# Branch B's scores: the second product of each head on 64 rows, side by side for two heads

## The chip, the cores and the metric

The kernel runs on one core of a Trainium2 chip. The metric is the time of one execution in microseconds of device time (median of the runs). Inputs and output are float32; TensorE gets its operands as float32r, split into a high part (rounded to float32r) and a low part (the remainder), so that a product of two values is made of several matmuls.

## The reference

One block of a bidirectional encoder, 1024 tokens of width 1024 and 16 meta tokens in front. Two attention branches read one normed input: branch A, differential attention over all tokens, and branch B, grouped-query attention in a window, with a sink logit for each head. Gates merge them, and a SwiGLU feed-forward follows. The change is in branch B's scores:

```
# 8 heads in 2 groups (g) of 4 (r), one key head per group, head width d = 64
s = einsum('bnqgrd,bnkgd->bngrqk', q, k) * d**-0.5 - slope * distance   # a block of 128 queries
s = where(visible, s, -inf)                                             # 3 blocks of keys + 16 meta keys
m = maximum(max(s), sink); p = exp(s - m)
y = einsum('bngrqk,bnkgd->bnqgrd', p / (sum(p) + exp(sink - m)), v)
```

## The kernel before

All engines' instructions are put in order by a scheduler that simulates the program when it is built; later stages fix TensorE's order by hand. The stages are: the input is loaded, normed and transposed (`turn_x`, through `transposed`, L154 to L165), with the first projections among the transposes; branch B's attention, woven into the projections of the rest (`project_steps`, L230); branch A's attention, woven into the gate projections (L881); then output projection and feed-forward. TensorE runs one instruction after another in the order that was built, so branch B's products stand between projection matmuls.

Branch B works on one group `g` and one tile `t` of 128 queries at a time (`attend_b`, L382): 2 groups by 8 tiles, 4 heads `r` in each. The keys of a tile are three blocks of 128 with the 16 meta keys behind each, 432 columns; the first and the last tile have two blocks, 288 columns.

Query and key have 64 values for each head, and the array has 128 rows, so high and low part share the rows. `qb[:, r]` holds the high part of head r's queries in rows 0 to 63 and the low part in rows 64 to 127. `kb[g][:, v]` holds the keys twice: for v = 0 high part above low part, for v = 1 low part above high part. Two matmuls of 128 rows, summed in one PSUM bank, thus give all four products of high and low parts. `kb_consume` (L305) and the `consume` of `qb_steps` (L367) copy the parts from a staging tile to these rows by DMA on SP's queue.

Each head's score goes to a bank of its own from a pair of banks under the tag "bs" (two buffers of one bank). VectorE's reduction (L399) adds the bias and takes the extreme value while it copies the score out; ScalarE's exponential (L403), GpSimd's scaling (L409), TensorE's transposes (L432) and the product with the values (L437) follow. `turn_x` uses the same two banks for the transposes of odd tiles, eight for each tile in two groups of four, and those of "bt" for the even tiles. The ninth tile holds the 16 meta tokens only, so its eight transposes have 16 rows.

Of the kernel before, what the change touches and what calls it, by code (L numbers as in the profile page):

```python
# [9 lines left out]
F32 = mybir.dt.float32  # L10
# [4 lines left out]
ALU = mybir.AluOpType  # L15
# [4 lines left out]
P = 128  # L20
# [54 lines left out]
def encoder_block(ctx: ExitStack, tc: tile.TileContext, x, meta, norm_mix, w_in, lq1, lk1, lq2, lk2,  # L75
                  subln, sink, w_ba, w_bb, w_o, norm_ffn, w_g, w_u, w_d, norm_final, out, dbg=None):
    nc = tc.nc
# [5 lines left out]
    def f32(ap):  # L83
        return ap.bitcast(F32)
# [13 lines left out]
    def bank(p, tag, name, bufs):  # L98
        return p.tile([P, 512], F32, tag=tag, name=name, bufs=bufs)
# [54 lines left out]
    def transposed(pp, xn, parts, hi, lo, at, name):  # L154

        highs = []
        for b in range(2):
            pt = pp(f"ptn_{name}_{b}").rearrange("p (c t) -> p c t", c=4)
            for c in range(4):
                k = 4 * b + c  # L160
                turned = nc.tensor.transpose(pt[:, c, :parts], xn[:parts, k * P:(k + 1) * P], ident[:parts, :parts])
            h = hi[:, 4 * b:4 * b + 4, at:at + parts]
            highs.append(nc.scalar.activation(h, pt[:, :, :parts], AF.Copy))
            low = nc.vector.tensor_tensor(lo[:, 4 * b:4 * b + 4, at:at + parts], pt[:, :, :parts], f32(h), ALU.subtract)
        return highs, low, turned  # L165
# [6 lines left out]
    psum1, close_psum1 = pool("psum1", space=PSUM)  # L172
# [4 lines left out]
    hT_hi = hpool.tile([P, DC, L_ROW], F32R, name="hT_hi")  # L177
    hT_lo = hpool.tile([P, DC, L_ROW], F32R, name="hT_lo")
# [33 lines left out]
    def ensure(n):  # L212
        while order and len(prepped) < n:
            col = order.pop(0)
            prepped[col] = prep(col, f"c{col}", lo_eng=nc.vector if col == C_QB else None)
# [73 lines left out]
    kb = [bpool.tile([P, 2, NT, 144], F32R, name=f"kb{g}") for g in range(BG)]  # L289
# [15 lines left out]
    def kb_consume(st, at, n):  # L305
        b0, nb = at // P, n // P
        for g in range(BG):
            rows = slice(64 * g, 64 * g + 64)
            for hl in range(2):
                for var, dst in ((0, slice(64 * hl, 64 * hl + 64)), (1, slice(64 - 64 * hl, 128 - 64 * hl))):  # L310
                    nc.sync.dma_start(f32(kb[g])[dst, var, b0:b0 + nb, 0:P],
                                      st[rows, hl, :nb * P].rearrange("p (b k) -> p b k", k=P))
                    if n % P:
                        nc.sync.dma_start(f32(kb[g])[dst, var, :, P:144],
                                          st[rows, hl, nb * P:n].unsqueeze(1).broadcast_to([64, NT, NM]))

    def vb_evac(pt, k0, nb, kp):
# [46 lines left out]
    def qb_steps(g, qb, jj):  # L364
        j = 2 * g + jj

        def consume(st, at, n):  # L367
            for par in range(2):
                for hl in range(2):
                    nc.sync.dma_start(f32(qb)[64 * hl:64 * hl + 64, 2 * jj + par, at:at + n],  # L370
                                      st[64 * par:64 * par + 64, hl, :n])
        return project_steps(C_QB + j * P, QB_CHUNKS if j < 2 else Q_CHUNKS, f"qb{j}", evac_split(qbs[:, j:j + 1], consume),
                             hi_first=j < 2)

    def project_qb(g, qb):
        for jj in range(2):
            ensure(1)
            for _ in qb_steps(g, qb, jj):
                pass
            ensure(W_BUFS - 1)  # L380

    def attend_b(g, t, qb):  # L382
        nm = f"{g}_{t}"
        b0, b1 = max(t - 1, 0), min(t + 2, NT)
        nb = b1 - b0
        W = nb * 144
        j0 = b0 - t + 1
        tb = tbx[:, j0:j0 + nb, :].rearrange("p j k -> p (j k)")
        st = bpool.tile([P, 4, 432], F32, tag="bs", name=f"bs_{nm}", bufs=2)
        mn = small.tile([P, 4], F32, tag="bmn", name=f"bmn_{nm}")  # L390
        dn = small.tile([P, 4], F32, tag="bdn", name=f"bdn_{nm}")
        es = small.tile([P, 4], F32, tag="bes", name=f"bes_{nm}")
        hs = slice(4 * g, 4 * g + 4)
        for r in range(4):
            ps = bank(psum1, "bs", f"bps_{nm}_{r}", 2)
            for v in range(2):
                nc.tensor.matmul(ps[:, :W], qb[:, r, t * P:(t + 1) * P],  # L397
                                 kb[g][:, v, b0:b1, :].rearrange("p b k -> p (b k)"), start=(v == 0), stop=(v == 1))
            nc.vector.tensor_tensor_reduce(st[:, r, :W], ps[:, :W], tb, 2.0 ** -(4 * g + r + 1), nsink[:, 4 * g + r:4 * g + r + 1],  # L399
                                           ALU.add, ALU.min, mn[:, r:r + 1])  # L400
        nc.vector.tensor_tensor(es, mn, sinkb[:, hs], ALU.add)
        for r in range(4):
            nc.scalar.activation(st[:, r, :W], st[:, r, :W], AF.Exp, bias=mn[:, r:r + 1], scale=-1.0,  # L403
                                 accum_out=dn[:, r:r + 1])
        nc.scalar.activation(es, es, AF.Exp)
        nc.vector.tensor_tensor(dn, dn, es, ALU.add)
        nc.vector.reciprocal(dn, dn)  # L407
        for r in range(4):
            scaled.append(nc.gpsimd.tensor_scalar(st[:, r, :W], st[:, r, :W], dn[:, r:r + 1], 1.0, ALU.mult, ALU.mult))  # L409

        md = mds[t % 2]
        own = (t - b0) * 144 + P
        nc.gpsimd.tensor_copy(md.rearrange("p (r a k) -> p r a k", r=4, a=2),
                              st[:, :, own:own + NM].unsqueeze(2).broadcast_to([P, 4, 2, NM]))

        def finish():
            py = bank(psum1, "by", f"bpy_{nm}", 1)
            for k in [8, *range(b0, b1)]:
                o = (k - b0) * 144
                pt = bank(psum1, "bt", f"bpt_{nm}_{k}", 2).rearrange("p (r t) -> p r t", r=4)  # L420
                if k == 8:
                    nc.tensor.transpose(pt[:, 0, :], md, ident)
                    tm = tms[t % 2]
                    hi = bpool.tile([P, P], F32R, tag="bmh", name=f"bmh_{nm}", bufs=1)
                    nc.scalar.activation(hi, pt[:, 0, :], AF.Copy, scale=of_hi)
                    for r in range(4):
                        at = slice(32 * r, 32 * r + 32)
                        nc.vector.scalar_tensor_tensor(tm[at, r], pt[at, 0, :], of_x[at], f32(hi[at]), ALU.mult, ALU.subtract)
                    nc.tensor.matmul(py, vb[g][:, 8, :], tm.rearrange("p r t -> p (r t)"), start=True, stop=False)
                    continue  # L430
                for r in range(4):
                    nc.tensor.transpose(pt[:, r, :], st[:, r, o:o + P], ident)  # L432
                tr = bpool.tile([P, 2, 4, P], F32R, tag="btr", name=f"btr_{nm}_{k}", bufs=4)
                nc.scalar.activation(tr[:, 0], pt, AF.Copy)
                nc.vector.tensor_tensor(tr[:, 1], pt, f32(tr[:, 0]), ALU.subtract)
                for hl in range(2):
                    nc.tensor.matmul(py, vb[g][:, k, :], tr[:, hl].rearrange("p r t -> p (r t)"),  # L437
                                     start=False, stop=(k == b1 - 1 and hl == 1))
            y1 = bpool.tile([64, 512], F32, tag="by1", name=f"by1_{nm}", bufs=2)
            nc.scalar.copy(y1, py[64:128])  # L440
            nc.vector.tensor_tensor(y1, py[0:64], y1, ALU.add)
            nc.sync.dma_start(yb_d[g][:, t * P:(t + 1) * P].rearrange("(r d) t -> d r t", r=4),
                              y1.rearrange("d (r t) -> d r t", r=4))
        return finish

    qb = new_qb(0)
# [6 lines left out]
    xts, xns, done, early = {}, {}, [], []  # L453
# [17 lines left out]

    def turn_x(t):
        parts = P if t < NT else NM
        return transposed(lambda name: bank(psum1, ("bt", "bs")[t % 2], name, 2), xns.pop(t), parts, hT_hi, hT_lo, t * P, f"a{t}")

    def advance(n):
        while n > 0 and early:
# [15 lines left out]
    rows = bpool.tile([DC, P], F32, tag="by1", name="gain_rows", bufs=2)  # L493
# [8 lines left out]
    for b in range(2):  # L502
        pt = pp_bank(f"gain_{b}")
        gain.append(pt)
        for c in range(4):
            k = 4 * b + c
# [14 lines left out]
    _, _, turned = turn_x(0)  # L521
# [4 lines left out]
    highs, low, _ = turn_x(1)  # L526
# [38 lines left out]
    product = advance(3 * DC)  # L565
# [4 lines left out]
    with tc.issue_after(product.ins):  # L570
        highs, _, _ = turn_x(4)
# [13 lines left out]
    highs, _, _ = turn_x(7)  # L585
    _, low, _ = turn_x(NT)
# [35 lines left out]
    nsink = acon.tile([P, BH], F32, name="nsink")  # L622
# [64 lines left out]
    for _ in range(QA_FIRST):  # L687
        product = next(qa0)
# [7 lines left out]
    qb = new_qb(1)  # L696
# [387 lines left out]
    for n in range(AH * NT + T_LAG):  # L1084
# [3 lines left out]
        if n < AH * NT:  # L1088
            h, t = divmod(n, NT)
# [178 lines left out]
    for o in range(DC):  # L1268
        w = first_w[o] if o < 2 else branch_w(ypool, o, w_bb, "b")
        for half in range(2):  # L1270
            gt, ps, tk = gated(0, o, half, w, yb)
# [599 lines left out]
```

## Time and profile before

| what | value |
|---|---|
| median of 3 runs | 1424.24 us (1422.53 to 1424.48) |
| the profiled execution | 1424.24 us, its span 1421.9 us |
| TensorE matmul busy | 1401.0 us, 99% of the span |
| VectorE, ScalarE, GpSimd busy | 914.8, 672.1, 636.7 us |
| branch B's score products (L397) | 128, from 62.1 to 269.7 us |

Rows of the timeline give an instruction's start and duration in us, engine, line, operation, output and inputs, the array's rows and columns in use (128\*128), the moving operand (128x432), and how many alike were merged (x2). PE is TensorE's matmul, PEld its weight load. A matmul's duration reaches into the next one's, as they are pipelined; the distance between starts says what one costs.

### The profile page before, as it was taken

The numbers are of one execution on the slowest core, as the hardware profiler recorded it, in microseconds if no ns is written. First come the engines' busy times: TensorE is split into PE (matmuls) and PEld (weight loads), VectorE is DVE, ScalarE is ACT, GpSimd is POOL, SyncE is SP. The second block draws the span as 40 slices with busy tenths as digits, with TensorE's granted clock in tenths as the row PEclk, the third lists the DMA queues.
The fourth block names the chain that finished last, engine by engine and source line by source line (L and its number), as shares of the span: only waits on it lengthen the run. The fifth ranks groups of instructions, "written<-read, shape, count | busy, mean of one in ns | idle before, by whom it ended". The sixth has DMA issues, their size and how long they took to land.

```text
span 1421.9 us, 20667 instructions
## 1 busy us (share of the span) xinstructions
PE 1401.0 (99%) x7183; PEld 1202.7 (85%) x7183; DVE 914.8 (64%) x1584; ACT 672.1 (47%) x1284; POOL 636.7 (45%) x648
## 2 busy tenths in 40 slices
PE   9999999998999999999999999999999999999998
PEld 8998999987888888878888888888888888888886
DVE  6555666527787878666978956544555453787566
ACT  6355556435445555455346644333333333444454
POOL 4156865546677666322503055555545441000442
PEclk9999999999999999999999999999999999999999
DMA  8446565386896363296522724433333323954343
GB/s 235 92 128 184 154 199 160 106 290 225 259 318 211 105 209 105 68 342 198 149 103 90 207 90 148 148 106 98 101 111 104 97 97 110 353 186 144 120 128 144
DMA packets 194297, 228.27 MB, mean 161 GB/s; under 512 B 16824, under 2 KB 127360, under 8 KB 194192
## 3 DMA queue, kind: packets, MB, share of 16 engines
q1 hardware_dynamic: 192272, 224.11, 49.3%
q10 hardware_dynamic: 1920, 2.83, 0.7%
q8 instruction: 57, 0.93, 0.3%
q14 instruction: 48, 0.39, 0.1%
HBM read 152.48 MB, written 67.86 MB: 155 GB/s over the span
## 4 chain that ended last, share of the span: by engine, by line
PE 90%; DVE 4%; DMA 2%; ACT 1%; issue 1%; SPq 1%; POOL 1%; ACTq 0%; POOLq 0%; DVEq 0%
PE pg L1634 29%; PE pd L1738 14%; PE pg L881 8%; PE ppa L721 6%; PE po L1537 4%; PE pp_va L230 3%; PE pp_ka L230 3%; PE aps L977 3%; PE pp_qa L230 3%; PE apy L1019 3%; PE pp_qb L230 3%; PE bps L397 2%; PE po L1545 2%; PE bpy L437 1%; PE apt L1006 1%; PE bpt L432 1%
## 5 line engine op out<-in xcount | busy, mean ns | idle before, releaser
L1634 PE MATMUL pg<-t,wop 128*128 128x512 f32 x1056 | 242.5, 389 | 0.0
L1634 PEld LDWEIGHTS pg<-t,wop 128*128 128x128 f32 x1056 | 198.3, 188 | 41.1
L120 POOL TENSOR_TENSOR wop<-wf,wop 128x512 fp32r<-128x512 f32 x114 | 153.9, 1351 | 162.4 <-ACT wop L119 148.7
L1738 PE MATMUL pd<-ob,oa 128*128 128x512 f32 x924 | 210.1, 390 | 0.2 <-DVE ob L120 0.2
L1738 PEld LDWEIGHTS pd<-ob,oa 128*128 128x128 f32 x924 | 173.4, 188 | 36.8 <-DVE ob L120 1.0
L1634 PE MATMUL pg<-b,wop 128*128 128x512 f32 x792 | 183.3, 390 | 0.0
L1634 PEld LDWEIGHTS pg<-b,wop 128*128 128x128 f32 x792 | 148.5, 188 | 30.7
L881 PE MATMUL pg<-hT_hi,wopg 128*128 128x512 f32 x448 | 169.9, 400 | 2.7 <-POOL wopg L800 1.8
L119 ACT ACTIVATE wop<-wf 128x512 fp32r<-128x512 f32 x128 | 80.8, 633 | 73.4 <-PE pg L1634 44.3
L120 POOL TENSOR_TENSOR oa<-ra,oa 128x512 fp32r<-128x512 f32 x27 | 34.9, 1294 | 169.4 <-ACT oa L119 167.7
L119 ACT ACTIVATE oa<-ra 128x512 fp32r<-128x512 f32 x77 | 48.7, 632 | 109.0 <-PE pd L1738 50.8
L988 ACT ACTIVATE as<-as,amn 128x1040 f32<-128x1040 f32 x64 | 74.5, 1165 | 50.6 <-DVE amn L984 50.4
L881 PEld LDWEIGHTS pg<-hT_hi,wopg 128*128 128x128 f32 x448 | 84.3, 188 | 15.5 <-POOL wopg L800 2.2
L1411 DVE TENSOR_TENSOR s<-wf,wf 128x512 f32<-128x512 f32 x22 | 17.6, 798 | 112.2 <-DMA wf<-in_w_ff_up_dram 70.7
L977 PE MATMUL aps<-ak,aq 128*128 128x352 f32 (+1 forms) x384 | 86.6, 334 | 2.4 <-DVE amn L980 2.2
L881 PE MATMUL pg<-hT_lo,wopg 128*128 128x512 f32 x224 | 88.2, 394 | 0.0
L980 DVE CUSTOM_DVE_ANT_0 as<-aps,dist,far_a 128x704 f32<-128x704 f32 x64 | 60.3, 943 | 34.9 <-PE aps L977 34.6
L399 DVE CUSTOM_DVE_ANT_0 bs<-bps,tbx,nsink 128x432 f32<-128x432 f32 (+1 forms) x64 | 38.6, 629 | 61.6 <-PE bps L397 37.8
L1009 ACT ACTIVATE at<-apt 128x512 fp32r<-128x512 f32 (+1 forms) x96 | 45.4, 484 | 63.0 <-PE apt L1006 63.0
L977 PEld LDWEIGHTS aps<-ak,aq 128*128 128x128 f32 x384 | 64.2, 189 | 12.2 <-DVE amn L980 4.7
L409 POOL TENSOR_SCALAR bs<-bs,bdn 128x432 f32<-128x432 f32 (+1 forms) x64 | 36.9, 596 | 75.3 <-DVE bdn L407 34.4
L1019 PEld LDWEIGHTS apy<-at,av 128*128 128x128 f32 x400 | 54.2, 190 | 4.0
(321 smaller groups left out, 3131.1 us busy)
## 6 DMA issues: line engine op xcount, KB each, us to landing
ra<-aop SPq DMA_DIRECT2D x77, 256.0 KB, 2.7
wf<-in_w_ff_gate_dram SPq DMA_DIRECT2D x25, 512.0 KB, 3.8
wf<-in_w_ff_up_dram SPq DMA_DIRECT2D x25, 512.0 KB, 3.8
aop<-as SPq DMA_DIRECT2D x44, 256.0 KB, 2.1
w_c<-in_w_in_dram SPq DMA_DIRECT2D x17, 512.0 KB, 4.8
aop<-c SPq DMA_DIRECT2D x33, 256.0 KB, 2.0
ak<-ka_d SPq DMA_DIRECT2D x16, 520.0 KB, 6.5
t_d<-tst SPq DMA_DIRECT2D x16, 512.0 KB, 3.8
```

The costliest lines, as they stand in the source:

```text
L119: high = nc.scalar.activation(hi, src, AF.Copy)
L120: lo_eng.tensor_tensor(lo, src, f32(hi), ALU.subtract)
L230: product = nc.tensor.matmul(ps[:, :n], a[:, c, :], b[:, c, at:at + n], start=(u == 0), stop=(u == 3 * DC - 1))
L721: nc.tensor.matmul(ps, w[:, a, j, :], src(j, b, tk), start=(j == 0 and n == 0), stop=(j == 3 and n == 2))
L881: nc.tensor.matmul(ps, op[:, x, c, :], h[:, 4 * d + c, HALF[t]], start=(p in (1, 6, 7) and c == 0 and i == 0), stop=(p in (2, 6, 3, 4) and ...
L977: nc.tensor.matmul(ps[:, :n], qs[m][:, t * P:(t + 1) * P], ks[m][:, vv, k0:k0 + n], start=(vv == 0), stop=(vv == 1))
L980: nc.vector.tensor_tensor_reduce(s[m][:, 0:2 * n].rearrange("p (a k) -> p a k", a=2), two[:, :, :n], dist[:, u0:u0 + 2 * n].rearrange("p ( ...
L988: nc.scalar.activation(s[m][:, 0:L], s[m][:, 0:L], AF.Exp, bias=mn[:, m, 1:2], scale=-1.0, accum_out=dn[:, 1:2] if m else first_sum)
L1019: nc.tensor.matmul(py[:, cols], v[:kp, a, k, :], at_[:kp, k, b, :], start=(k == 0 and j == 0), stop=(k == 8))
L1537: nc.tensor.matmul(sets_o[p][u], oa[:, a, u * P:(u + 1) * P], ob[:, b, :], start=(p in (1, 5) and j == 0 and k == 0), stop=(p in (2, 3) an ...
L1634: nc.tensor.matmul(ps, op[:, x, c, :], b[:, y, c, :], start=(p in (1, 5) and c == 0 and n == 0), stop=(p in (4, 2, 3) and c == 3 and n == ...
L1738: nc.tensor.matmul(ps[u], oa[:, a, u * P:(u + 1) * P], ob[:, b, :], start=(p in (1, 2, 5) and j == 0 and k == 0), stop=(p in (2, 3, 4) and ...
```

## The change

Both variants of `kb` now hold one part in both halves of the rows: v = 0 the high part twice, v = 1 the low part twice. `qb` keeps high above low for even heads and has low above high for odd ones (row = 64 * (hl ^ par)). So the first product of a head, with 128 rows, gives high times high and low times high. The second takes only the 64 rows with the query's high part against the keys' low part: rows 0 to 63 for even heads, rows 64 to 127 for odd ones. The product of low and low part is left out.

The heads are taken in pairs, each pair with one buffer of two banks (`two_banks`, one buffer under the tag "bs"): first product of the even head, first of the odd one, second of the even one, second of the odd one, each asked to be issued behind the one before. Two reductions follow. `turn_x` takes its two banks for an odd tile from the same buffer. The number of matmuls, reductions and DMAs stays.

```diff
             for hl in range(2):
-                for var, dst in ((0, slice(64 * hl, 64 * hl + 64)), (1, slice(64 - 64 * hl, 128 - 64 * hl))):
-                    nc.sync.dma_start(f32(kb[g])[dst, var, b0:b0 + nb, 0:P],
+                for dst in (slice(0, 64), slice(64, 128)):
+                    nc.sync.dma_start(f32(kb[g])[dst, hl, b0:b0 + nb, 0:P],
                                       st[rows, hl, :nb * P].rearrange("p (b k) -> p b k", k=P))
...
                 for hl in range(2):
-                    nc.sync.dma_start(f32(qb)[64 * hl:64 * hl + 64, 2 * jj + par, at:at + n],
+                    row = 64 * (hl ^ par)
+                    nc.sync.dma_start(f32(qb)[row:row + 64, 2 * jj + par, at:at + n],
                                       st[64 * par:64 * par + 64, hl, :n])
...
+    def two_banks(name):
+        return psum1.tile([P, 2, 512], F32, tag="bs", name=name, bufs=1)
...
-        for r in range(4):
-            ps = bank(psum1, "bs", f"bps_{nm}_{r}", 2)
+        for pair in range(2):
+            two = two_banks(f"bps_{nm}_{pair}")
+            product = None
             for v in range(2):
-                nc.tensor.matmul(ps[:, :W], qb[:, r, t * P:(t + 1) * P],
-                                 kb[g][:, v, b0:b1, :].rearrange("p b k -> p (b k)"), start=(v == 0), stop=(v == 1))
-            nc.vector.tensor_tensor_reduce(st[:, r, :W], ps[:, :W], tb, 2.0 ** -(4 * g + r + 1), nsink[:, 4 * g + r:4 * g + r + 1],
-                                           ALU.add, ALU.min, mn[:, r:r + 1])
+                for par in range(2):
+                    rows = slice(64 * par, 64 * par + 64) if v else slice(0, P)
+                    with ExitStack() as adjoining:
+                        if product is not None:
+                            adjoining.enter_context(tc.high_priority())
+                            adjoining.enter_context(tc.issue_after(product.ins))
+                        product = nc.tensor.matmul(two[:, par, :W], qb[rows, 2 * pair + par, t * P:(t + 1) * P],
+                                                   kb[g][rows, v, b0:b1, :].rearrange("p b k -> p (b k)"),
+                                                   start=(v == 0), stop=(v == 1))
+            for par in range(2):
+                r = 2 * pair + par
+                nc.vector.tensor_tensor_reduce(st[:, r, :W], two[:, par, :W], tb, 2.0 ** -(4 * g + r + 1),
+                                               nsink[:, 4 * g + r:4 * g + r + 1], ALU.add, ALU.min, mn[:, r:r + 1])
...
-        return transposed(lambda name: bank(psum1, ("bt", "bs")[t % 2], name, 2), xns.pop(t), parts, hT_hi, hT_lo, t * P, f"a{t}")
+        if t % 2:
+            two = two_banks(f"ptn_{t}")
+            halves = iter((two[:, 0], two[:, 1]))
+        return transposed(lambda name: next(halves) if t % 2 else bank(psum1, "bt", name, 2), xns.pop(t), parts, hT_hi, hT_lo,
+                          t * P, f"a{t}")
```

More of the change, by code (lines that the diff above doesn't have):

```diff
@@ L309, in kb_consume @@
             for hl in range(2):
-                for var, dst in ((0, slice(64 * hl, 64 * hl + 64)), (1, slice(64 - 64 * hl, 128 - 64 * hl))):
-                    nc.sync.dma_start(f32(kb[g])[dst, var, b0:b0 + nb, 0:P],
+                for dst in (slice(0, 64), slice(64, 128)):
+                    nc.sync.dma_start(f32(kb[g])[dst, hl, b0:b0 + nb, 0:P],
                                       st[rows, hl, :nb * P].rearrange("p (b k) -> p b k", k=P))
                     if n % P:
-                        nc.sync.dma_start(f32(kb[g])[dst, var, :, P:144],
+                        nc.sync.dma_start(f32(kb[g])[dst, hl, :, P:144],
                                           st[rows, hl, nb * P:n].unsqueeze(1).broadcast_to([64, NT, NM]))
```

## The prediction

> **What bounds the kernel now.** I read the head of the page first, then the chain that ended last.
>
> ```profile
> span 1421.9 us, 20667 instructions
> ...
> PE 1401.0 (99%) x7183; PEld 1202.7 (85%) x7183; DVE 914.8 (64%) x1584; ACT 672.1 (47%) x1284; POOL 636.7 (45%) x648
> ...
> PE 90%; DVE 4%; DMA 2%; ACT 1%; issue 1%; SPq 1%; POOL 1%; ACTq 0%; POOLq 0%; DVEq 0%
> ```
>
> TensorE carries 90% of the chain. An average says little about one stage, so next come stage sums: branch B's scores run from 62 to 271 us, the last projections to 324, and then branch A begins.
>
> ```profile
> core 0: us, PE busy (x) PEld busy (x) DVE busy (x) ACT busy (x) POOL busy (x), PEclk, DMA share, GB/s
> ...
> 62.00:271.00 209.00, 209.00 (x1196) 189.93 (x1195) 122.86 (x322) 118.06 (x284) 128.90 (x128) 1.00 0.55 159
> 271.00:324.00 53.00, 52.76 (x296) 47.19 (x294) 21.57 (x48) 19.75 (x40) 25.43 (x39) 1.00 0.70 236
> ```
>
> In the score stage TensorE is busy 209.00 of 209.00 us at the full granted clock (1.00), and no other compute engine exceeds 128.90. So a TensorE slot saved or added there moves the end of the stage one for one. Behind it TensorE idles for only 0.24 us to 324; the loads of branch A wait for buffers that this stage gives back, so they move with it, and I let nothing be absorbed. The groups of the score line give its size:
>
> ```profile
> L397 PE MATMUL bps<-kb,qb x128: 289/356/446, 62.1 to 269.7; 128*128 128x432 f32 x96, 128*128 128x288 f32 x32
> ```
>
> There are 128 products, 96 wide (432 columns) and 32 narrow (288).
>
> **The price of one product.** The 356 ns overlap the next matmul, so a product's real cost is the distance between starts, in the timeline:
>
> ```profile
> 122.46 0.55 PE L397 MATMUL bps<-kb,qb 128*128 128x432 f32 x2
> 122.84 0.40 PE L230 MATMUL pp_qa<-hT_hi,wl_c 128*128 128x512 f32 x1
> ...
> 151.69 0.42 PE L397 MATMUL bps<-kb,qb 128*128 128x288 f32 x2
> 151.95 0.40 PE L230 MATMUL pp_qb<-hT_hi,wl_c 128*128 128x512 f32 x1
> ```
>
> Two wide products take 122.84 - 122.46 = 0.38 us, so 0.19 each; two narrow ones 151.95 - 151.69 = 0.26, so 0.13 each.
>
> **What the change does to it.** The number of matmuls stays. Per head one product keeps 128 rows, the other has 64; of two neighbouring heads one uses rows 0 to 63, the other 64 to 127, into different banks, and they are issued next to each other. If the array runs them side by side, a pair of heads has three slots where it had four. There are 32 pairs, 24 wide and 8 narrow: 24 x 0.19 + 8 x 0.13 = 5.6 us would go.
>
> Against it stands the array's change to 64 rows and back, 33 times: in the built order the four products of a pair stand together in 31 pairs, and in the very first pair the two 64-row products stand apart, so each makes a visit of its own. No 64-row matmul is in this trace, but the nearest thing is: the transposes of the 16 meta rows, twice four, between full matmuls of 256 columns. I take these as the price.
>
> ```profile
> 37.95 0.28 PE L230 MATMUL pp_qb<-hT_lo,wh_c 128*128 128x256 f32 x1
> 38.07 0.28 PE L230 MATMUL pp_qb<-hT_hi,wl_c 128*128 128x256 f32 x1
> 38.28 0.42 PE L161 MATMUL ptn_a<-ident,xn_a 16*128 16x16 f32 x4
> 38.63 0.38 PE L230 MATMUL pp_qb<-hT_hi,wh_c 128*128 128x256 f32 x1
> 38.94 0.41 PE L161 MATMUL ptn_a<-ident,xn_a 16*128 16x16 f32 x4
> 39.28 0.38 PE L230 MATMUL pp_qb<-hT_lo,wh_c 128*128 128x256 f32 x1
> 39.51 0.28 PE L230 MATMUL pp_qb<-hT_hi,wl_c 128*128 128x256 f32 x1
> ```
>
> Shorter windows split the groups of four: the last three of the first visit and the last one of the second.
>
> ```profile
> 38.37 0.33 PE L161 MATMUL ptn_a<-ident,xn_a 16*128 16x16 f32 x3
> ...
> 39.15 0.21 PE L161 MATMUL ptn_a<-ident,xn_a 16*128 16x16 f32 x1
> ```
>
> And the weight loads:
>
> ```profile
> 38.28 0.32 PEld L161 LDWEIGHTS ptn_a<-ident,xn_a 16*128 16x128 f32 x4
> ...
> 39.28 0.19 PEld L230 LDWEIGHTS pp_qb<-hT_lo,wh_c 128*128 128x128 f32 x1
> 39.39 0.19 PEld L230 LDWEIGHTS pp_qb<-hT_hi,wl_c 128*128 128x128 f32 x1
> ```
>
> Undisturbed, the starts are 38.07 - 37.95 = 0.12 apart. Now step by step:
> - Weights in the open. After the visit the load starts at 39.28 together with its matmul, not a matmul ahead, and the next start comes at 39.51, 0.23 later: 0.11 is added, which is also the distance of the loads, 39.39 - 39.28.
> - Entry, the gap. The matmul at 38.07 would have ended its stream at 38.19; the 16-row one starts at 38.28, 0.09 later. Second visit: 38.63 + 0.11 + 0.12 = 38.86, start at 38.94, 0.08 later. I take 0.09.
> - Entry, the load. It starts at 38.28 as its matmul does, so it lies in the open too. Its price is between 0.02, by which the first small matmul (38.37 - 38.28 = 0.09) lasts longer than its followers (0.07, next step), and the 0.11 above. The score weights have the 128 columns and the kind of data of the full loads: 0.11.
> - Exit. From the last small matmul to the next weight load 39.28 - 39.15 = 0.13. Inside the visit the small ones stand (39.15 - 38.94)/3 = 0.07 apart, so the switch alone costs between 0.06 and 0.13. I take 0.09, the entry's price.
>
> That it is the row change, and not the transposing, two controls show:
>
> ```profile
> 36.65 0.27 PE L161 MATMUL ptn_a<-ident,xn_a 128*128 128x128 f32 x1
> 36.68 0.36 PE L230 MATMUL pp_qb<-hT_hi,wh_c 128*128 128x256 f32 x1
> ...
> 36.65 0.19 PEld L230 LDWEIGHTS pp_qb<-hT_hi,wh_c 128*128 128x128 f32 x1
> ...
> 109.66 0.28 PE L230 MATMUL pp_ka<-hT_hi,wh_c 128*128 128x272 f32 x1
> 109.67 0.09 PEld L276 LDWEIGHTS pv_va<-ident,vt_va 128*32 128x32 f32 x1
> 109.78 0.27 PE L276 MATMUL pv_va<-ident,vt_va 128*32 128x128 f32 x1
> ```
>
> Out of a 128-row transpose the next weights load with its start (36.65 both); into a 32-column one they load 0.01 after the matmul before started, and it follows 0.12 later. Neither pays a gap.
>
> The Trainium skill, "TensorEngine Tiling (Array Packing)", Key Properties, says that a change of tiling mode drains TensorE; the visits agree with some 0.09 us each way, while the 32-column control, a change of mode too, shows no drain. By that rule, with no price for the loads, the sum would be less than mine.
>
> The 64-row stretch itself: the first product streams 0.19 (wide). How much later the second starts is in no row. Lower bound 0, both loads at once; upper bound 0.11, its load waiting for the first one's. Its rows are others than the first one's, so it lies nearer to a matmul whose weights don't stand in line: the one at 36.68 follows its transpose (36.65) by 0.03. I take 0.03. "TensorE: Matmul & The Clock Gate" of the Trainium skill, Part 3, has packed matmuls start some 4 ns apart; by it the sum would be about 0.8 us lower.
>
> So the two second products of a pair:
> - wide: 0.09 + 0.11 + 0.19 + 0.03 + 0.09 + 0.11 = 0.62 where they took 0.38: +0.24, x 24 = +5.8
> - narrow: 0.09 + 0.11 + 0.13 + 0.03 + 0.09 + 0.11 = 0.56 where they took 0.26: +0.30, x 7 = +2.1
> - the first pair: 2 x (0.09 + 0.11 + 0.13 + 0.09 + 0.11) = 1.06 for 0.26: +0.8
>
> Sum +8.7 us. With all low bounds (entry load 0.02, exit 0.06, second start 0) it is 24 x 0.09 + 7 x 0.15 + 0.6 = +3.8; with the high ones (exit 0.13, second start 0.11) 24 x 0.36 + 7 x 0.42 + 0.9 = +12.5.
>
> **The rest of the edit.** The two score banks become one buffer, so a pair's first product waits until both reductions of the pair before are done; behind it on TensorE stand the projections that fill the stage.
>
> ```profile
> 118.02 0.67 DVE L399 CUSTOM_DVE_ANT_0 bs<-bps,tbx,nsink 128x432 f32<-128x432 f32 x1 [2.68 <-PE bps L397]
> ```
>
> Two reductions take 2 x 0.67 = 1.3 us. In the built order at least 19 other matmuls lie between two pairs; at the 0.13 of the narrow products, 2.5 us or more: nothing. If that cover were gone, see the third rival. The copies that fill kb and qb keep number and size, only their target rows differ: nothing. The odd tiles' first transposes share the one buffer too, and the scheduler spreads them among the first projections: within 0.5 us, either way, as no row prices it. From the end of the stage on, TensorE's order is the same as before.
>
> The profiled execution took 1424.24 us (2.3 outside the span), which is also the median. Forecast: 1424.24 + 8.7 = 1432.9 us.
>
> **Rivals.**
> - *Faster: no gap at a switch to 64 rows*, the drain being a matter of 16 of 32 rows. The 32-column control speaks for it, four gaps at two visits, equal within 0.05, against it. Then 5.6 us go: 1418.6. The Trainium skill, "TensorE: Matmul & The Clock Gate", Part 3, gives 3.07 times the speed for four packed row tiles and names no gap, which points this way. Decided by whether the 64-row weights load ahead. Chance 0.10.
> - *A wash: drains, but loads ahead.* A wide pair takes 0.09 + 0.19 + 0.09 = 0.37 for 0.38, a narrow one 0.31 for 0.26: 24 x -0.01 + 8 x 0.05 = +0.2, 1424.4. Against it: both visits load in the open. 0.06.
> - *The single score buffer becomes the bound.* If the reductions stand behind other VectorE work, a pair waits. One 0.67 reduction at half of 31 hand-overs is +10 on top: about 1443. It decides once reductions end later than the next pair's place. The 2.5 us between pairs in the built order speak against it. 0.04.
> - *No overlap of the 64-row products* (the change doesn't do what it says): second start 0.19 or 0.13 later, 24 x 0.40 + 7 x 0.40 + 0.8 = +13.2: 1437.4. 0.06.
>
> **How the numbers follow.** The forecast keeps 0.74; its own range is 1428.0 to 1436.7. The range leaves out the faster case, the wash and the buffer case (0.20 together) and takes in the bounds, half a microsecond for the order, and the case without overlap: 1427.5 to 1438.0. About 0.2% (2.8 us) is what a measurement of this kernel can tell from no change. Faster 0.10; same 0.07, the wash and a sliver of the forecast; slower 0.83.
>
> **What would show it.** Right: at each pair the first 64-row weight load starts about 0.09 after the stream before it ends and not a matmul ahead, the two 64-row matmuls start within 0.11 of each other, the next full load again stands with its matmul, and 62 to 271 stretches by about 9 us with TensorE still busy throughout. Wrong: 64-row loads ahead of time (the wash or the faster rival), starts 0.19 apart (no overlap), or TensorE idle in front of a pair (the buffer).

## The result, and the profile after

| | us |
|---|---|
| before, median of 4 runs | 1423.89 (1422.53 to 1424.48) |
| changed, median of 4 runs | 1435.46 (1434.13 to 1438.74) |
| ratio, 95% interval | 1.0086 (1.0067 to 1.0105) |
| forecast | 1432.9 (1427.5 to 1438.0) |

The change costs 11.6 us by the medians. The profiled execution of the changed kernel is the longest of its four, 1438.74 us, 3.3 above their median; its start, shown below, is one place where it can have lost them.

The head of the page and the chain, changed kernel:

```profile
span 1436.6 us, 20656 instructions
...
PE 1413.5 (98%) x7183; PEld 1200.1 (84%) x7183; DVE 917.9 (64%) x1584; ACT 672.5 (47%) x1284; POOL 635.6 (44%) x648
...
PE 92%; DVE 4%; ACT 1%; DMA 1%; issue 1%; ACTq 0%; SPq 0%; DVEq 0%
```

The same 7183 matmuls keep TensorE busy for 12.5 us longer. The sums by stretch, in the columns of the prediction's table, show where:

```profile
core 0: us, PE busy (x) PEld busy (x) DVE busy (x) ACT busy (x) POOL busy (x), PEclk, DMA share, GB/s
10.00:20.00 10.00, 8.02 (x41) 7.41 (x42) 7.33 (x9) 6.90 (x13) 5.00 (x5) 0.66 0.81 269
62.00:271.00 209.00, 209.00 (x1160) 178.35 (x1159) 115.05 (x294) 109.51 (x262) 122.64 (x122) 1.00 0.53 152
271.00:324.00 53.00, 50.94 (x282) 44.81 (x281) 22.18 (x54) 20.87 (x49) 25.01 (x37) 0.97 0.56 175
```

Three things differ from before. In the score stage TensorE is as full as it was (209.00 of 209.00), but does 1160 matmuls where it did 1196: nothing waits, the score products take longer. Behind it TensorE now idles, at a granted clock of 0.97. And at the start, a stretch that the forecast gave half a microsecond, the clock is down. Before, that stretch reads:

```profile
10.00:20.00 10.00, 9.73 (x80) 9.28 (x79) 9.17 (x14) 7.94 (x15) 6.49 (x7) 1.00 1.09 321
```

**A visit to 64 rows.** The timeline of one pair in the changed kernel; the third row is from a shorter window, which splits the group of four above it:

```profile
132.88 0.39 PE L230 MATMUL pp_qa<-hT_hi,wh_c 128*128 128x512 f32 x1
133.11 0.94 PE L408 MATMUL bps<-kb,qb 128*128 128x432 f32 x4
133.59 0.47 PE L408 MATMUL bps<-kb,qb 64*128 64x432 f32 x2
133.98 0.50 PE L230 MATMUL pp_qa<-hT_lo,wh_c 128*128 128x512 f32 x1
134.32 0.40 PE L230 MATMUL pp_qa<-hT_hi,wl_c 128*128 128x512 f32 x1
```

And its weight loads:

```profile
133.59 0.19 PEld L408 LDWEIGHTS bps<-kb,qb 64*128 64x128 f32 x2 [0.28 <-issue]
133.98 0.19 PEld L230 LDWEIGHTS pp_qa<-hT_lo,wh_c 128*128 128x128 f32 x1 [0.21 <-issue]
```

The rows are read so. Two full products begin at 133.11, 0.19 each, and end at 133.49; the 64-row load begins at 133.59: a gap of 0.09 to 0.10. Load and matmul stand together, so the load is in the open. The two 64-row matmuls take 0.47 together, first start to last end, where a single one's record is 0.46 (it contains its load): they run side by side. The next full load begins at 133.98, 0.39 on: 0.11 for the load, 0.19 for the stream, 0.09 for the way back. It too stands with its matmul, which is followed after 134.32 - 133.98 = 0.34 instead of the 0.23 of its neighbours (133.11 - 132.88): another 0.11. So the two second products cost 0.09 + 0.39 + 0.11 = 0.59 where they had cost 0.38. Of the visit's steps only the second start differs from its price: it costs nothing.

**The start.** First TensorE before, then the changed kernel:

```profile
9.14 1.05 PE L161 MATMUL ptn_a<-ident,xn_a 128*128 128x128 f32 x8
10.43 1.23 PE L230 MATMUL pp_kb<-hT_hi,wh_c 128*128 128x256 f32 x8 [0.24 <-ACT hT_hi L163]
...
51.81 0.44 PE L230 MATMUL pp_vb<-hT_hi,wh_c 128*128 128x384 f32 x1 [0.26 <-DVE qk_stage L254]
```

```profile
8.91 0.60 PE L161 MATMUL ptn<-ident,xn_a 128*128 128x128 f32 x4
11.09 0.74 PE L230 MATMUL pp_kb<-hT_hi,wh_c 128*128 128x256 f32 x4 [1.58 <-ACT hT_hi L163]
11.30 0.68 DVE L164 TENSOR_TENSOR hT_lo<-ptn,hT_hi 128x512 fp32r<-128x512 f32 x1
12.03 0.95 PE L161 MATMUL ptn<-ident,xn_a 128*128 128x128 f32 x4 [0.21 <-DVE hT_lo L164]
13.67 1.22 PE L230 MATMUL pp_kb<-hT_hi,wh_c 128*128 128x256 f32 x4 [0.69 <-ACT hT_hi L163]
14.69 0.41 PE L230 MATMUL pp_kb<-hT_lo,wh_c 128*128 128x256 f32 x1
14.90 0.41 PE L230 MATMUL pp_kb<-hT_hi,wl_c 128*128 128x256 f32 x1
...
57.46 0.44 PE L230 MATMUL pp_vb<-hT_hi,wh_c 128*128 128x384 f32 x1
```

Before, the eight transposes of tile 1 go in one piece, four into each bank. Now the second four start at 12.03, when VectorE has read the first four (11.30 + 0.68 = 11.98), although they go to the other bank. The buffer of two banks is kept as one tile, and a write to one half of it waited for the reads of the other half. TensorE idles 1.58, 0.21 and 0.69 us, and from 12.3 to 19.1 us the granted clock is halved: the projections stand 0.21 apart (14.90 - 14.69) where 0.12 is usual. The first `pp_vb` comes 5.65 us later than before.

Not all of the 5.65 us is the buffer's. ScalarE's copies into `hT_hi` stand behind its copy of a weight, and in this execution that weight came in later than before (first row before, second row changed):

```profile
7.67 1.06 ACT L119 ACTIVATE wh_c<-w_c 128x1024 fp32r<-128x1024 f32 x1 [0.63 <-DMA w_c<-in_w_in_dram]
...
8.52 1.06 ACT L119 ACTIVATE wh_c<-w_c 128x1024 fp32r<-128x1024 f32 x1 [1.74 <-DMA w_c<-in_w_in_dram]
```

In experiment 2, with the same buffer, this copy starts at 7.46 and the wait of 1.58 is 0.69. The clock's part is 0.34 x 10 = 3.4 us at most.

**The end of branch B.** TensorE's last products of branch B now stand behind the last projection, in the changed kernel:

```profile
304.61 0.28 PE L230 MATMUL pp_ka<-hT_hi,wl_c 128*128 128x272 f32 x1
...
306.48 0.51 PE L451 MATMUL bpy<-btr,vb 128*128 128x512 f32 x1 [0.45 <-ACT btr L448]
307.20 0.50 PE L451 MATMUL bpy<-btr,vb 128*128 128x512 f32 x1 [0.22 <-DVE btr L449]
309.09 0.71 PE L899 MATMUL pg<-hT_hi,wopg 128*128 128x512 f32 x1 [1.39 <-DVE by L455]
```

Before, the projections cover them, but 45 us on a wait for a gate weight follows, which the changed kernel no longer has:

```profile
293.40 0.29 PE L230 MATMUL pp_ka<-hT_hi,wl_c 128*128 128x272 f32 x1
293.52 0.39 PE L881 MATMUL pg<-hT_hi,wopg 128*128 128x512 f32 x1
...
338.89 0.51 PE L881 MATMUL pg<-hT_hi,wopg 128*128 128x512 f32 x1 [1.76 <-POOL wopg L800]
```

So 0.45 + 0.22 + 1.39 = 2.06 us are lost at the border of the two branches, and the wait of 1.76 behind it is gone. The clock falls behind these waits too in this execution (0.74 from 310 to 315 us). From the first gate projection to the end of the span it is 1436.6 - 309.09 = 1127.5 us, before 1421.9 - 293.52 = 1128.4.

### The profile page after: what moved, and what is told of

It is laid out like the page before. It is cut to its first block, busy times and chain, and to the rows that moved or that the text cites. A ratio compares the mean times of both kernels' runs of the same rounds, so it can differ in the third digit from the quotient of the medians.

```text
span 1436.6 us, 20656 instructions
## 1 busy us (share of the span) xinstructions
PE 1413.5 (98%) x7183; PEld 1200.1 (84%) x7183; DVE 917.9 (64%) x1584; ACT 672.5 (47%) x1284; POOL 635.6 (44%) x648
## 4 chain that ended last, share of the span: by engine, by line
PE 92%; DVE 4%; ACT 1%; DMA 1%; issue 1%; ACTq 0%; SPq 0%; DVEq 0%
PE pg L1652 29%; PE pd L1756 15%; PE pg L899 9%; PE ppa L739 6%; PE po L1555 4%; PE aps L995 3%; PE pp_ka L230 3%; PE pp_va L230 3%; PE pp_qa L230 3%; PE apy L1037 3%; PE pp_qb L230 3%; PE bps L408 2%; PE bpy L451 2%; PE apt L1024 2%; PE po L1563 2%; PE bpt L446 1%
## 5 line engine op out<-in xcount | busy, mean ns | idle before, releaser
L120 POOL TENSOR_TENSOR wop<-wf,wop 128x512 fp32r<-128x512 f32 x114 | 150.7, 1322 | 164.3 <-ACT wop L119 154.3
```

What stands on the lines that cost most here:

```text
L120: lo_eng.tensor_tensor(lo, src, f32(hi), ALU.subtract)
```

## The experiments

The theory: the switch to 64 rows and back costs more than the shared slot saves (about 7 to 9 us), and the buffer of two banks costs the rest. Rivals: the buffer or the order of the pairs makes most of it; or the 64-row products don't overlap.

**1. The buffer taken out** (`e1_single_banks`). The changed kernel with the two single banks of before, for scores and transposes:

```diff
-            two = two_banks(f"bps_{nm}_{pair}")
+            two = [bank(psum1, "bs", f"bps_{nm}_{2 * pair + par}", 2) for par in range(2)]
...
-        if t % 2:
-            two = two_banks(f"ptn_{t}")
...
+        return transposed(lambda name: bank(psum1, ("bt", "bs")[t % 2], name, 2), xns.pop(t), parts, hT_hi, hT_lo, t * P, f"a{t}")
```

> The 64-row pairs stay, but scores and odd tiles' transposes get the two single banks of before. Theory (three costs: switches to 64 rows about +7.8 us, the two-bank buffer's delay of the odd transposes at the start, its delay of branch B's end): the start is as before (first pp_vb near 52 us), 62 to 271 us stays full, the switches remain: 1431.5 to 1434 us. Rival (all of the loss is the buffer's, switches are free): 1418.6 us with overlap, 1424 us without.

Measured 1431.26 us, 0.2 below the expected range, ratio to before 1.0058 (1.0043 to 1.0073). Most of the loss stays without the buffer. Its timeline at the points used above:

```profile
52.52 0.44 PE L230 MATMUL pp_vb<-hT_hi,wh_c 128*128 128x384 f32 x1 [0.25 <-DVE qk_stage L254]
...
303.80 0.50 PE L892 MATMUL pg<-hT_hi,wopg 128*128 128x512 f32 x1 [1.39 <-DVE by L452]
```

The start is nearly that of before (52.52 for 51.81). From there to the first gate projection it takes 303.80 - 52.52 = 251.28, the changed kernel 309.09 - 57.46 = 251.63, the kernel before 293.52 - 51.81 = 241.71. So the buffer costs at most 0.35 us in the score stage, and what it costs lies ahead of the first `pp_vb`.

**2. The buffer alone** (`e2_full_rows`). Buffer and pairs as changed, but all products on 128 rows; four terms are computed again. The rest of the edit, not shown, puts the parts in `kb` and `qb` back in their old places:

```diff
-                    rows = slice(64 * par, 64 * par + 64) if v else slice(0, P)
+                    rows = slice(0, P)
```

> The two-bank buffer and the pairs' order stay, but all products have 128 rows as before, four terms. Theory: no gaps inside a pair, four starts 0.19 us apart; the start is late by 2 to 6 us and branch B ends behind the last projection by some 2 us: 1427 to 1431 us. Rival (all of the loss is the buffer's): 1435 us. Rival (all of it is the switches'): 1424 us.

Measured 1427.5 us, ratio 1.0032 (1.0018 to 1.0045). The score stage is then that of before, the start is not:

```profile
10.00:20.00 10.00, 8.92 (x71) 8.48 (x72) 7.35 (x9) 7.57 (x14) 5.07 (x6) 1.00 0.84 277
62.00:271.00 209.00, 209.00 (x1196) 190.72 (x1195) 116.68 (x304) 114.68 (x273) 126.29 (x123) 1.00 0.54 159
```

It does 1196 matmuls in the stage again. In this execution the clock is not halved at the start, so the halving comes in only some executions of such a start. Without it the first `pp_vb` is 54.14 - 51.81 = 2.33 us later than before, and the waits are 0.69 (below), 0.16 and 0.69:

```profile
10.23 0.74 PE L230 MATMUL pp_kb<-hT_hi,wh_c 128*128 128x256 f32 x4 [0.69 <-ACT hT_hi L163]
...
54.14 0.44 PE L230 MATMUL pp_vb<-hT_hi,wh_c 128*128 128x384 f32 x1
```

**3. Neither** (`e6_pairs_single_full`). Experiment 1 with all products on 128 rows (all four terms); of the change the order of the pairs is left, and the places of the parts in `kb` and `qb`:

```diff
-                    rows = slice(64 * par, 64 * par + 64) if v else slice(0, P)
+                    rows = slice(0, P)
```

> As e1_single_banks, with the pairs' order, the new layout and the single banks, but every product on 128 rows: the second one gives query high and low times key low, so four terms as before. Theory (switches and the two-bank buffer are all there is): within 1.5 us of before, 1422.5 to 1425 us, the rest being branch B's end behind the last projection. Rival (the pairs' order itself costs): 1427 us or above, which would take as much off the switches' share of e1_single_banks.

Measured 1425.18 us, ratio 1.0007 (0.9997 to 1.0016), slightly above what was expected, and not told apart from no change. Its rows at the two points:

```profile
51.55 0.34 PE L230 MATMUL pp_vb<-hT_hi,wh_c 128*128 128x384 f32 x1
...
295.41 0.50 PE L892 MATMUL pg<-hT_hi,wopg 128*128 128x512 f32 x1 [1.39 <-DVE by L452]
```

The border shows the wait of 1.39 as in experiment 1. Between the points lie 295.41 - 51.55 = 243.86 us, in experiment 1 251.28: that the second products use 64 rows costs 7.42 us there, with all else alike. The kernel before takes 241.71; the 2.15 us more come with the order of the pairs, 0.23 + 1.39 of them as waits at the border, and are in part made good behind it (1422.8 - 295.41 = 1127.4 us to the end, before 1128.4).

The four make a square of ratios (experiment 2 has the old places in `kb` and `qb`, the other three the new ones):

| | one buffer of two banks | two single banks | difference |
|---|---|---|---|
| second products on 64 rows | 1.0086 (the change) | 1.0058 | 0.0028 |
| all on 128 rows | 1.0032 | 1.0007 | 0.0025 |
| difference | 0.0054 | 0.0051 | |

At 1423.9 us the 64 rows cost 7.3 to 7.7 us, the buffer 3.6 to 4.0, the pairs' order (with the places) 1.0. Rows and columns add up, which gives no sign that the two feed on each other; but the intervals of the cells (0.0010 to 0.0019 either way) leave 2 to 4 us either way on each difference.

**4. No overlap** (`e3_same_rows`). The kernel of experiment 1 with both second products of a pair on rows 0 to 63:

```diff
-                    row = 64 * (hl ^ par)
+                    row = 64 * hl
...
-                    rows = slice(64 * par, 64 * par + 64) if v else slice(0, P)
+                    rows = slice(0, 64) if v else slice(0, P)
```

> As e1_single_banks, but the second products of both heads of a pair use rows 0 to 63. Theory (different rows run side by side): the second start comes a whole stream later, 0.19 us wide and 0.13 narrow: 24 x 0.19 + 8 x 0.13 = 5.6 us over e1_single_banks, less 0.4 for one switch fewer. Rival (no side by side run in float32r, or the pair is bound by its two weight loads): within 1 us of e1_single_banks.

Measured 1437.33 us, 6.1 above experiment 1. Its weight loads at a wide pair:

```profile
129.32 0.29 PEld L405 LDWEIGHTS bps<-kb,qb 64*128 64x128 f32 x2 [0.33 <-issue]
129.92 0.19 PEld L230 LDWEIGHTS pp_qa<-hT_hi,wl_c 128*128 128x128 f32 x1 [0.30 <-issue]
```

From the first 64-row load to the next full one it takes 0.60, with the rows apart 0.39: one slot more. From the first `pp_vb` (52.20) to the first gate projection (308.48) it takes 256.28 us, 5.0 more than experiment 1. So the overlap is real and worth 5 to 6 us here, where the forecast had 5.6 (and 5.2 was expected of this kernel, with one switch fewer); the switches eat more than that.

**5. Twice the visits** (`e4_two_visits`). Experiment 1 with each second product right behind its own first, so every product makes a visit of its own (64 instead of 33):

```diff
-            for v in range(2):
-                for par in range(2):
+            for par in range(2):
+                for v in range(2):
```

> As e1_single_banks, but each head's second product stands right behind its own first one: 64 switches to 64 rows and back where there were 33. Theory (a visit costs about 0.09 + 0.11 on the way in and 0.10 + 0.11 on the way out, beside its stream): a wide pair takes 2 x 0.60 for 0.60, a narrow one 2 x 0.53 for 0.53: 24 x 0.60 + 7 x 0.53 = 18 us over e1_single_banks. Rival (switches are free, the loss lies elsewhere): 5.6 us over it, the lost overlap alone.

Measured 1448.43 us, 17.2 above experiment 1, where 18 was expected. Its loads in one narrow pair, from short windows:

```profile
174.04 0.18 PEld L405 LDWEIGHTS bps<-kb,qb 64*128 64x128 f32 x1 [0.21 <-issue]
...
174.37 0.19 PEld L405 LDWEIGHTS bps<-kb,qb 128*128 128x128 f32 x1
...
174.70 0.18 PEld L405 LDWEIGHTS bps<-kb,qb 64*128 64x128 f32 x1
...
175.03 0.19 PEld L230 LDWEIGHTS pp_va<-hT_lo,wh_c 128*128 128x128 f32 x1
```

Every change of rows stands 0.33 behind the one before, whichever way it goes: 0.13 for the stream, 0.20 to 0.21 for gap and open load. The time follows the number of visits and of slots.

**6. More work in a visit** (`e5_twice_inside`). Experiment 1 with the pair of 64-row products issued twice inside the visit, so the low parts of the keys are counted twice:

```diff
-            for v in range(2):
+            for v in range(3):
...
-                                                   kb[g][rows, v, b0:b1, :].rearrange("p b k -> p (b k)"),
-                                                   start=(v == 0), stop=(v == 1))
+                                                   kb[g][rows, min(v, 1), b0:b1, :].rearrange("p b k -> p (b k)"),
+                                                   start=(v == 0), stop=(v == 2))
```

> As e1_single_banks, but each pair's two 64-row products are issued twice inside the same visit (the low parts of the keys are counted twice). Theory (the price of a visit is fixed, a further pair of side by side products adds one stream): 24 x 0.19 + 8 x 0.13 = 5.6 us over e1_single_banks, or some 4 if branch B no longer ends behind the last projection, as in this order: 1435 to 1437 us. Rival (every 64-row product pays a load or a gap of its own): 3 to 6 us more, 1439 us or above.

Measured 1439.42 us, ratio 1.0106 (1.0089 to 1.0122), 6.8 us above experiment 1 by the ratios. A visit's loads:

```profile
128.62 0.30 PEld L405 LDWEIGHTS bps<-kb,qb 64*128 64x128 f32 x4 [0.33 <-issue]
129.21 0.19 PEld L230 LDWEIGHTS pp_qa<-hT_lo,wh_c 128*128 128x128 f32 x1 [0.30 <-issue]
```

All four 64-row loads are done in 0.30, so the second two run ahead of their matmuls again, and the visit lasts 0.59 where it lasted 0.39: 0.20 for one more pair, one slot. That makes 24 x 0.20 + 8 x 0.13 = 5.8 us. The time itself lies above what the theory expected (1435 to 1437) and in the rival's range (1439 or above); the trace decides. From the first `pp_vb` (51.95) to the first gate projection (307.06) it takes 255.11 us, 3.83 more than experiment 1, which idles 0.23 + 1.39 at its border where this kernel doesn't wait: 5.45 us for the products, about one slot for each pair. The rest came behind the first gate projection, among it a wait of 1.30 for a gate weight that experiment 1 doesn't have, and is not explained in full. So the fixed price hangs on the visit, not on the products in it.

**7. Scores on the buffer, transposes off it** (`e7_turns_on_bt`). The changed kernel with all tiles' transposes on the banks of "bt":

```diff
-        if t % 2:
-            two = two_banks(f"ptn_{t}")
...
+        return transposed(lambda name: bank(psum1, "bt", name, 2), xns.pop(t), parts, hT_hi, hT_lo, t * P, f"a{t}")
```

> The changed kernel, with the transposes of all tiles on the two banks that the even tiles use; the scores keep the two-bank buffer and the 64-row pairs. Theory (the buffer costs at the start alone, where an odd tile's second four transposes wait for the first four to be copied out): the start is as before, first pp_vb near 52 us, 1431 to 1432.5 us. Rival (the buffer costs in the score stage): as the changed kernel, 1435 us.

Measured 1437.58 us, ratio 1.0093 (1.0077 to 1.0108): a miss. One pair of banks for all tiles delays the start too, at other places: the first `pp_vb` comes at 57.36, 5.55 us later than before, with the clock at 1.00. The waits of TensorE in the first 62 us of this kernel (total, times, longest):

```profile
PE ptn_a L161 <- DVE hT_lo L164: 1.9, 3, 0.9
PE pp_vb L230 <- DVE qk_stage L254: 1.8, 1, 1.8
PE pp_kb L230 <- ACT hT_hi L163: 1.6, 1, 1.6
```

It tells nothing on the price of the start, so that was put into the kernel before instead.

**8. The start alone** (`e8_start_alone`). The kernel before, with one edit: both groups of an odd tile's transposes go through one bank, the second behind the reads of the first.

```diff
-        return transposed(lambda name: bank(psum1, ("bt", "bs")[t % 2], name, 2), xns.pop(t), parts, hT_hi, hT_lo, t * P, f"a{t}")
+        one = bank(psum1, "bs", f"ptn_{t}", 2) if t % 2 else None
+        return transposed(lambda name: one if t % 2 else bank(psum1, "bt", name, 2), xns.pop(t), parts, hT_hi, hT_lo, t * P, f"a{t}")
```

> The kernel before, with one edit: an odd tile's two groups of four transposes share one bank, so the second group waits until the first is copied out, as the two-bank buffer makes it wait in the changed kernel. Scores are those of before. Theory (the waits at the start are what separates the changed kernel from e1_single_banks, about 4 us): 1426 to 1429 us, the first pp_vb 2 to 5.6 us later than before. Rival (the waits are covered by other work at the start, and the 4 us belong to the scores' buffer): 1424 us.

Measured 1427.43 us, ratio 1.0023 (1.0013 to 1.0034): 3.3 us, with no other part of the change. Consecutive odd tiles still take turns at two banks here, which they don't in the changed kernel. The timeline shows the same kind of waits (0.69 twice, 0.16, where the changed kernel had 1.58, 0.21 and 0.69), the sums the clock:

```profile
10.51 0.74 PE L230 MATMUL pp_kb<-hT_hi,wh_c 128*128 128x256 f32 x4 [0.69 <-ACT hT_hi L163]
11.41 0.66 PE L161 MATMUL ptn<-ident,xn_a 128*128 128x128 f32 x4 [0.16 <-DVE hT_lo L164]
12.75 1.09 PE L230 MATMUL pp_kb<-hT_hi,wh_c 128*128 128x256 f32 x4 [0.69 <-ACT hT_hi L163]
...
55.67 0.44 PE L230 MATMUL pp_vb<-hT_hi,wh_c 128*128 128x384 f32 x1
```

```profile
10.00:20.00 10.00, 8.64 (x56) 8.21 (x57) 7.35 (x10) 6.51 (x12) 5.13 (x6) 0.83 0.86 280
```

The first `pp_vb` is 3.86 late, in an execution that is 2.4 us above the median of this kernel; the clock can make up 0.17 x 10 = 1.7 us of it. Experiment 2 has the same three waits, the clock at 1.00, and is 2.33 late. From there to the first gate projection (297.37) it takes 241.70 us, as before (241.71). So the buffer's price lies at the start; how it divides between the waits and the clock over many executions is not settled.

## Why the prediction was right, and where it was off

The forecast was 2.6 us below the median measured, with its mechanism confirmed and one term far too small. There is some luck in how near it came: the switches were put 1.0 to 1.4 us too high, which hides a part of what the sum left out.

- *The switch, step by step: right.* Predicted 0.62 for a wide visit, found 0.59. The gaps (0.09 each way) and the open loads (0.11 each), taken from 16-row transposes, hold for 64-row products. The second start was sized at 0.03 and is nothing, the two products starting together. So a wide pair pays 0.21 instead of 0.24. The sum was 8.7 us, and with 0 for the 31 second starts 7.8; the traces of experiments 1 and 3 give 7.4, the square of ratios 7.3 to 7.7. "TensorE: Matmul & The Clock Gate" of the Trainium skill, Part 3, whose 4 ns between starts was set beside the 0.03, agrees with the trace, where the shortest windows place the two starts at 133.586 and 133.590; its speed-up for packed tiles names no gap, and here the gaps and the loads behind them (0.40) outweigh the overlap (0.19).
- *The stage is bound by TensorE: right.* 209.00 of 209.00 us busy, before and after.
- *The single buffer in the score stage: nothing, right.* 251.63 us from the first `pp_vb` to the gates with it, 251.28 without; the waits at the border (2.06 and 1.62) differ by about as much.
- *"Within 0.5 us, either way" for the odd tiles' transposes: wrong, 3.3 us* (experiment 8), 3.6 to 4.0 by the square. This is the term that was mis-sized. The step saw that the transposes share one buffer, and left out that the second four then wait for the reads of the first four. The waits at the start are 1.5 us in experiment 8 and 2.5 in the changed kernel, where a late weight adds to them, and in both the clock is lower behind them.
- *"From the end of the stage on, TensorE's order is the same" and "I let nothing be absorbed": both wrong, and the two errors nearly cancel.* The last products of branch B fell behind the last projection (2.06 us of idle time), and the wait of 1.76 us for a gate weight is gone. That the order of the pairs nets to 1.0 us is the square's reading; its interval includes zero.

Summed: 7.3 for the switches (experiments 1 and 3), 3.3 for the start (experiment 8), 1.0 for the order (experiment 3) make 11.6. The medians differ by as much; with intervals of 2 us and more on the parts, so close an agreement is chance. The ratio of 1.0086 gives 12.2 (9.5 to 15.0). The rivals fall: no gap and loads ahead by the rows of the visit, the buffer as a bound by 251.63 against 251.28, no overlap by experiment 4.

## What to carry to other kernels

Two 64-row matmuls side by side save one slot, but the visit among full matmuls has a fixed price: here 0.40 us, two gaps of 0.09 and two loads of 0.11 in the open, against 0.19 saved by a wide pair, so that, as an estimate from these rows, three pairs or more per visit would be needed (it wasn't tried: a group has four heads, two pairs, and even these would need more banks for their scores at once). Price a change of the rows in use from the nearest small matmul in the trace, weight loads included. And when two buffers become one tile of two banks, look at every user of it, not only at the one that the change is about: the price came from the transposes, tens of microseconds ahead of the scores.

## What the runs showed of the hardware that was not expected

- Behind a few short waits the granted clock was halved in some executions and not in others. In the changed kernel's profiled execution, waits of 1.58 and 0.21 us from 9 us on are followed by a clock of 0.50 from 12.3 to 19.1 us (mean 0.66 from 10 to 20 us); in experiment 8, waits of 0.69, 0.16 and 0.69 by a mean of 0.83; in experiment 2, with the same three waits, it stayed at 1.00. At the border, with a last wait of 1.39 in each, it is 0.97 from 271 to 324 us in the changed kernel and 1.00 in experiment 1. So the waits don't settle it alone, that they are the cause is not shown, and how much of the price of the buffer is the clock's stays open.
- The gap at a change of rows is about 0.09 us for 64 rows, both ways, as for the 16 rows before, and two loads for different halves of the rows take no longer than one (0.19).
